# A decoder layer's output projection as seven half-size products

## The chip, the cores and the metric

The kernel runs on one NeuronCore of a Trainium2 chip. The metric is the device time of one execution in microseconds, the median of several. TensorE is PE below (PEld is its weight load), VectorE DVE, ScalarE ACT, GpSimd POOL, and SyncE, which issues most DMAs, SP.

## The reference, cut

One layer of a decoder for 1024 positions of 1024 channels in float32. Two gated feed-forward parts stand around a mixer of three branches, whose gated sum goes through one output projection.

```python
x = x + 0.5 * swiglu(rmsnorm(x, ffn1_norm), ffn1_w_gu, ffn1_w_down)
h = rmsnorm(x, mix_norm)
z = h @ w_in
...
merged = (gates[:, :, 0] * (y_a @ w_branch_a)
          + gates[:, :, 1] * (y_b @ w_branch_b)
          + gates[:, :, 2] * (y_c @ w_branch_c))
x = x + merged @ w_out
x = x + 0.5 * swiglu(rmsnorm(x, ffn2_norm), ffn2_w_gu, ffn2_w_down)
```

## The kernel before

**Layout.** Channels lie on the 128 partitions and positions along the free dimension: a matrix of 1024 x 1024 is eight row tiles `d` (or `c`) of 128 channels, each in two halves `half` (or `f`) of 512 positions. A float32 product is made of three matmuls of rounded parts (`mm3`, line 145): each operand is split into a high part (a cast on ACT, line 134) and a low part (a subtraction on DVE, line 135), and hi x hi, hi x lo and lo x hi are summed in one PSUM bank. One `mm3` is three matmuls of 128x128 by 128x512.

**Stages.** `run` (line 1008) goes through the first feed-forward part, the input projection with its gates (`Gates.run`, line 1513), the mixer (line 916: branch A, branch C, the attention of branch B, then branch B's product), the output projection (`project`, line 978), and the second feed-forward part. The feed-forward parts and the gates already use seven products of half-size blocks in place of eight (`Seven`, line 1171): with blocks of weights a11, a12, a21, a22 and of operands b11, b21, ..., sums s1 to s4 of weights and t1 to t4 of operands are made first, and seven products are added into the four blocks of the result.

**Branch B and the projection.** At the end of the mixer, for each row tile d and half f, four `mm3` (`branch`, line 551) make one bank. DVE multiplies it with the gate (`bsig`, line 973), POOL adds the sum of the other two branches (`bm`, line 974), and the result is split into `merged[f][d]`, which lies in the 16 `h` buffers. `project` then makes, for each half and each of eight columns c, a sum over eight `mm3` in one bank, adds it to the residual row (line 989), feeds the square into the norm's sum (`norm.feed`: a square on ACT, an addition on DVE, line 358) and stores the row. `w_out` is loaded and split twice, once for each half. After half 0, four tasks are put between the columns of half 1: the token sums (line 361), the turning of the scale (line 373), and the norm and split of half 0's rows.

**The second feed-forward part** begins with `units` (line 1283): for three units (two columns of weights each) the products s3·t3 and s4·b22, which need half 0 alone, are made first, while half 1's sums, scale and operands are made.

**What sets the order.** In a `manual_schedule` block the engines named keep the program's order. Elsewhere, in the mixer and in `project` among others, the compiler's planner orders each engine's instructions by its own estimate of when each is ready, program order breaking ties. Buffers come from pools: a tile asks for any free buffer of its tag, and waits if none is free. The pools here: `h` 16 and `x` (`x4`) 10 buffers of 128x1024; `raw` 3, `whi` and `wlo` 5 each of the same size; `t` (`row`) 6 of 128x512; `w4` 11 of 128x1024, in the feed-forward parts alone; PSUM has 4 single banks `one` and 4 `bank`. The attention's output keeps 8 of the 10 `x` buffers until branch B's product has ended. All the loads in this part go through SP's queue in order.

Of the kernel before, what the change touches and what calls it, by code (L numbers as in the profile page):

```python
# [9 lines left out]
F32 = mybir.dt.float32  # L10
F32R = mybir.dt.float32r
# [6 lines left out]
P = 128  # L18
# [31 lines left out]
class Kernel:  # L50
# [35 lines left out]
    def wide(self, tag):  # L86
        return self.wp.tile([P, D], F32R, name=tag, tag=tag, bufs=5)
# [828 lines left out]
    def mixer(self, norm):  # L916
# [45 lines left out]
        merged = [self.hrows() for _ in range(2)]  # L962
        with tc.tile_pool(name="bp", bufs=4) as p:
            w = {}
            for d, f in [(d, f) for d in range(DT - 3) for f in range(2)] + [(d, f) for f in range(2) for d in range(DT - 3, DT)]:
                if d not in w:
                    w[d] = self.load(a["w_branch"][1, d])
                sig, m = (p.tile([P, 512], F32, name=n) for n in ("bsig", "bm"))
                nc.sync.dma_start(sig, self.sig[DT + d][:, f])
                nc.sync.dma_start(m, mc[d, f])  # L970
                b = self.bank()
                self.branch(b, w[d], yb, f)
                nc.vector.tensor_tensor(sig, sig, b, op=ALU.mult)
                nc.gpsimd.tensor_tensor(sig, sig, m, op=ALU.add)
                self.split(*merged[f][d], sig)
        return merged

    def project(self, merged, norm, sink):

        nc, a = self.nc, self.a  # L980
        tasks = []
        for half in range(2):
            for c in range(DT):
                w = self.load(a["w_out"][c])
                b = self.bank()
                for k in range(DT):
                    self.mm3(b, w[k], merged[half][k], k == 0, k == DT - 1)
                x = norm.x(half, c)
                nc.vector.tensor_tensor(x, x, b, op=ALU.add)
                norm.feed(half, c)  # L990
                sink(half, c)
                if tasks:
                    tasks.pop(0)()
            tasks = norm.first() if half == 0 else tasks
        for t in tasks:
            t()
# [11 lines left out]
    def run(self):  # L1008
# [38 lines left out]
        with self.banks("mixps") as self.pm:  # L1047
            merged = self.mixer(norm)
        with tc.tile_pool(name="f2", bufs=1) as fp, self.banks("f2ps") as self.pm:
            rows = Rows(self)  # L1050
            for half in range(2):
                for p in range(DT // 2):
                    nc.sync.dma_start(rows.take(half, p), x1d[half, p])
            norm = OpNorm(self, rows, lambda: self.g_ffn2)
            ffn = SwiGLU(self, a["ffn2_w_gu"], a["ffn2_w_down"], fp, norm, 2)
            for f in range(2):
                ffn.fetch(f, [ffn.w4] * 4)
            ffn.fetch(2, [ffn.w4, self.x4] * 2)
            self.project(merged, norm, lambda half, c: keep(x2d, norm.t, half, c))
            E = mybir.EngineType  # L1060
            with tc.manual_schedule(engines={E.PE, E.DVE, E.Activation}):
                t1 = [ffn.w4] * 3 + [self.x4]
                ffn.units(
                    (0, 1), extra=2, kinds=(self.single, self.single, self.bank, self.bank, self.bank),
                    late=1, turn=2, rooms=lambda dt: t1.pop(0)(dt))
# [22 lines left out]
class OpNorm:  # L1088
# [11 lines left out]
    def feed(self, half, c):  # L1100
        self.acc[half] = self.k.norm_feed(self.acc.get(half), self.x(half, c), 512)
# [69 lines left out]
class Seven:  # L1171
# [54 lines left out]
    def product(self, out, w, name, op, first=True):  # L1226
        for j in range(4):
            m = tuple(x[:, j % 2] for x in self.norm.op[op][j // 2])
            s = tuple(x[:, j * P:(j + 1) * P] for x in w[name])
            self.k.mm3(out, s, m, first and j == 0, j == 3, skip_group_check=True)  # L1230

# [729 lines left out]
```

## Time and profile before

| | us |
|---|---|
| median of 3 runs | 2208.12 |
| lowest, highest | 2205.59, 2212.95 |
| the profiled execution, its own time | 2207.62 |
| the span of its trace | 2205.5 |

The trace is of one execution, the one of 2207.62 us; about 2.1 us of it lie outside the span. The page gives the busy time of each engine. A matmul's duration (0.39 us) overlaps that of the next, so that PE's pace is read from the starts. In a row of the timeline stand the start, the duration, the engine, the line, the operation, out<-in by name, the sizes, the count merged, and in brackets the idle time before it with what ended it. In a row of a group stand the count, then the busy time and the mean of one in ns, then the idle time before. In the list of DMAs the last figures are the size of one and the median time from issue to landing.

Branch B's product is at 1437.8 to some 1481 us of the trace, the projection from there to 1570.1, and the second feed-forward part follows.

### The profile page before, as it was taken

What the parts mean: (1) busy time and instruction counts of PE and PEld (TensorE: products, weight loads), DVE (VectorE), ACT (ScalarE), POOL (GpSimd) and SP (SyncE); (2) the same over time, 40 slices, a digit from 0 to 9 for tenths busy, and PEclk for the clock granted to TensorE, in tenths of its full rate; (3) what the DMA queues carried; (4) which work ended last, traced back from release to release, by engine and by line L of the source; (5) the groups of instructions that cost most, each with busy time, mean ns of one, the idle gap of its engine ahead of it and who ended that gap; (6) DMA issues with size and microseconds to landing.
All of it is one profiled execution on the core that took longest, in us unless ns stands there. A gap on an engine that the chain in (4) does not pass through costs nothing.

```text
span 2205.5 us, 27222 instructions
## 1 busy us (share of the span) xinstructions
PE 2176.3 (99%) x10192; PEld 1806.9 (82%) x10192; DVE 1536.0 (70%) x2252; ACT 901.5 (41%) x1385; POOL 243.3 (11%) x250
## 2 busy tenths in 40 slices
PE   8999999999999999999999999999999999999999
PEld 4778888888888888888878879988888888888887
DVE  7966566569889547555687779876886665656964
ACT  5432222233445335432366459833432222224332
POOL 0121212110000000000001431140021121211000
PEclk9999999999999999999999999999999999999999
DMA  4243333394432353324345660076033233338442
GB/s 154 69 133 95 115 101 113 108 330 147 149 123 94 117 172 116 133 96 148 114 149 194 190 222 31 28 259 251 29 115 115 91 110 101 115 122 322 138 139 95
DMA packets 124627, 300.05 MB, mean 136 GB/s; under 512 B 14096, under 2 KB 22288, under 8 KB 124496
## 3 DMA queue, kind: packets, MB, share of 16 engines
q1 hardware_dynamic: 121808, 295.17, 40.2%
q10 hardware_dynamic: 2688, 3.15, 0.4%
q8 instruction: 80, 1.31, 0.3%
q14 instruction: 51, 0.42, 0.1%
HBM read 209.01 MB, written 89.26 MB: 135 GB/s over the span
## 4 chain that ended last, share of the span: by engine, by line
PE 87%; DVE 9%; DMA 2%; issue 1%; ACT 1%; POOL 0%; SPq 0%; POOLq 0%; DVEq 0%; ACTq 0%
PE one L148 14%; PE one L150 14%; PE one L149 14%; PE bank L150 11%; PE bank L148 11%; PE bank L149 11%; DVE wlo L135 2%; PE mm L148 2%; PE mm L150 2%; PE mm L149 2%; PE bank L856 1%; PE bank L871 1%; PE bank L872 1%; DVE h L135 1%; PE bank L406 1%
## 5 line engine op out<-in xcount | busy, mean ns | idle before, releaser
L134 ACT CAST whi<-x 128x1024 fp32r<-128x1024 f32 (+1 forms) x213 | 200.6, 947 | 527.6 <-PE one L149 223.7
L1233 DVE TENSOR_TENSOR t<-t,one 128x512 f32<-128x512 f32 x149 | 102.3, 687 | 256.3 <-PE one L150 256.2
L148 PE MATMUL bank<-h,whi 128*128 128x512 f32 x688 | 268.9, 392 | 2.1 <-ACT t L1259 1.7
L150 PE MATMUL bank<-h,wlo 128*128 128x512 f32 x688 | 268.6, 391 | 0.0
L149 PE MATMUL bank<-h,whi 128*128 128x512 f32 x688 | 268.6, 390 | 0.0
L135 DVE TENSOR_TENSOR wlo<-x,whi 128x1024 fp32r<-128x1024 f32 (+1 forms) x213 | 234.0, 1102 | 39.5 <-ACT whi L134 39.3
L135 DVE TENSOR_TENSOR wlo<-w,whi 128x1024 fp32r<-128x1024 f32 (+1 forms) x153 | 168.4, 1115 | 75.5 <-ACT whi L134 75.4
L134 ACT CAST whi<-w 128x1024 fp32r<-128x1024 f32 (+1 forms) x153 | 142.6, 955 | 175.3 <-PE one L149 107.9
L148 PE MATMUL one<-h,whi 128*128 128x512 f32 x496 | 194.2, 392 | 1.8 <-ACT t L1259 1.2
L150 PE MATMUL one<-h,wlo 128*128 128x512 f32 x496 | 193.2, 389 | 0.5 <-DVE wlo L135 0.5
L149 PE MATMUL one<-h,whi 128*128 128x512 f32 x496 | 193.0, 389 | 0.0
L150 PE MATMUL one<-w,wlo 128*128 128x512 f32 x432 | 168.4, 390 | 0.4 <-DVE wlo L135 0.4
L148 PE MATMUL one<-w,whi 128*128 128x512 f32 x432 | 168.5, 390 | 0.0
L1233 DVE TENSOR_TENSOR raw<-t,one 128x512 f32<-128x512 f32 x130 | 89.2, 687 | 105.1 <-PE one L150 99.7
L148 PEld LDWEIGHTS bank<-h,whi 128*128 128x128 f32 x688 | 129.6, 188 | 29.2 <-ACT t L1259 2.2
L150 PEld LDWEIGHTS bank<-h,wlo 128*128 128x128 f32 x688 | 129.5, 188 | 27.0
L149 PEld LDWEIGHTS bank<-h,whi 128*128 128x128 f32 x688 | 129.5, 188 | 26.5
L1710 POOL TENSOR_TENSOR raw<-raw 128x512 f32<-128x512 f32 x39 | 81.1, 2078 | 591.4 <-DVE raw L1569 346.4
L148 PE MATMUL one<-whi 128*128 128x512 f32 x368 | 143.4, 390 | 0.0
L149 PE MATMUL one<-wlo,whi 128*128 128x512 f32 x368 | 143.2, 389 | 0.0
L150 PE MATMUL one<-whi,wlo 128*128 128x512 f32 x368 | 143.2, 389 | 0.0
L149 PE MATMUL one<-w,whi 128*128 128x512 f32 x356 | 138.5, 389 | 0.0
(364 smaller groups left out, 4701.2 us busy)
## 6 DMA issues: line engine op xcount, KB each, us to landing
x<-in_ffn_w_gu_dram SPq DMA_DIRECT2D x76, 512.0 KB, 4.4
w<-tdt SPq DMA_DIRECT2D x40, 512.0 KB, 3.7
gate<-raw SPq DMA_DIRECT2D x36, 512.0 KB, 3.0
tdb<-raw SPq DMA_DIRECT2D x64, 256.0 KB, 2.0
w<-tdb SPq DMA_DIRECT2D x30, 512.0 KB, 6.8
h<-in_ffn_w_down_dram SPq DMA_DIRECT2D x28, 512.0 KB, 6.3
x<-in_w_in_dram SPq DMA_DIRECT2D x26, 512.0 KB, 6.2
tdt<-w SPq DMA_DIRECT2D x44, 256.0 KB, 2.0
```

The lines of the kernel that those rows point to most:

```text
L134: self.nc.scalar.copy(hi, src)
L135: return (eng or self.nc.vector).tensor_tensor(lo, src, hi.bitcast(F32), op=ALU.subtract)
L148: mmul(out, s[0], m[0], start=first, stop=False, **kw)
L149: mmul(out, s[0], m[1], start=False, stop=False, **kw)
L150: self.last = mmul(out, s[1], m[0], start=False, stop=last, **kw)
L406: nc.tensor.transpose(b[:m, k * P:(k + 1) * P], s, self.ident)
L856: nc.tensor.transpose(b[:, at:at + P], prs[t][:, kk * P:(kk + 1) * P], self.ident)
L871: nc.tensor.matmul(o, w, pt[0], start=n == 0, stop=False)
L872: nc.tensor.matmul(o, w, pt[1], start=False, stop=n == len(pts) - 1)
L1233: return self.nc.vector.tensor_tensor(out, x, y, op=ALU.add)
L1710: sub = lambda d, x, y: nc.gpsimd.tensor_tensor(d, x, y, op=ALU.subtract)
```

## The change

The output projection becomes seven products of half-size blocks over all row tiles. The two dimensions that are halved are the 1024 channels summed over (row tiles j and j + 4) and, in the result, the columns c and c + 4; the operand's two halves of positions f are its two block columns. Each product is four outputs u of four `mm3`, 16 `mm3`.

- **Weight sums.** `out_sums` is called after gate units 4, 5, 6 and 7. It loads two column tiles of `w_out`, makes s1 to s4 on POOL, stores s2 and s3 in DRAM as they are, splits s1 and s4 on ACT and DVE, and stores their parts.
- **Branch B** moves into the scope of the second feed-forward part. `branch_b` goes over four pairs of row tiles j and j + 4. It loads the branch's weights for both tiles at once, in a `whi` buffer. After the pair's half 0 the operands b11 and b21 are split into `w4` buffers; after half 1, POOL makes two differences, DVE one, and t2, t3, t4, t1 and b22 are split.
- **`project`** makes a11·b11, a12·b21, s2·t2, s3·t3, a22·t4 (the last in `close`), then s1·t1 and s4·b22 by column. The first, third, fourth and fifth share four `one` banks, which hold running sums that are added to the rows after each product. The weights are asked for some pairs ahead. The second feed-forward part's loads, weight sums and splits are put between the products.
- **`close`** lies in the hand-ordered block: the fifth product, and the last two with half 0's token sums, scale, norm and operands between them. The square sums of most rows are added on POOL in place of DVE.
- **`units`** opens in another order, s4·b22 of two units first, and half 1's token sums stand in the middle of the second product.

```diff
+    def branch_b(self, yb, mc, w4):
...
+        op = {n: [None] * 4 for n in ("b11", "b21", "t1", "t2", "t3", "t4", "b22")}
+        rooms = iter([self.x4, self.x4, self.raw, self.raw, self.raw, self.x4, self.x4, self.raw])
+        rooms2 = iter([w4, w4, w4, self.x4])
...
+        def put(room, src, *names):
+            hi, lo = room(F32R), room(F32R)
+            self.split(hi, lo, src)
+            for i, n in enumerate(names):
+                op[n][j] = hi[:, i], lo[:, i]
+
+        for j in range(4):
+            raw = self.wide("whi", F32)
...
+            hi, lo = self.wide("whi"), self.wide("wlo")
+            self.split(hi, lo, raw)
+            s = []
+            for f in range(2):
+                s.append(two(next(rooms)()))
+                for i in range(2):
+                    d = j + 4 * i
+                    x, m = s[f][:, i], self.row()
+                    nc.sync.dma_start(x, self.sig[DT + d][:, f])
+                    nc.sync.dma_start(m, mc[d, f])
+                    b = self.bank()
...
+                    nc.vector.tensor_tensor(x, x, b, op=ALU.mult)
+                    nc.gpsimd.tensor_tensor(x, x, m, op=ALU.add)
+                if f == 0:
+                    put(w4, s[0], "b11", "b21")
+            if j % 2 == 0:
+                t2 = [next(rooms2)(F32R) for _ in range(2)]
+            t = self.row()
+            nc.gpsimd.tensor_tensor(s[1][:, 0], s[1][:, 0], s[0][:, 0], op=ALU.subtract)
+            nc.gpsimd.tensor_tensor(t, s[1][:, 1], s[1][:, 0], op=ALU.subtract)
+            nc.vector.tensor_tensor(s[0], s[0], t.unsqueeze(1).to_broadcast([P, 2, 512]), op=ALU.subtract)
+            op["t2"][j] = tuple(x[:, j % 2] for x in t2)
+            self.split(*op["t2"][j], t)
+            put(self.h4, s[0], "t3", "t4")
+            put(self.h4, s[1], "t1", "b22")
...
+        def product(out, n, u, t, first=False, mid=None):
+            while todo and (u % 2 == 0 and todo[0] in ahead[n, u // 2] or (n, u) not in ws):
+                weights(*todo.pop(0))
+            w = ws.pop((n, u))
+            for j in range(4):
+                self.mm3(
+                    out, tuple(x[:, j * P:(j + 1) * P] for x in w), op[t][j],
+                    first and j == 0, j == 3, skip_group_check=True)
...
+        def add(half, c, b, last=False, eng=nc.gpsimd):
+            x = norm.x(half, c)
+            nc.vector.tensor_tensor(x, x, b, op=ALU.add)
+            if last:
+                norm.feed(half, c, eng)
                 sink(half, c)
...
+        p = [self.single() for _ in range(4)]
+        for u in range(4):
+            product(p[u], "a11", u, "b11", True)
+            add(0, u, p[u])
+        for u in range(4):
+            b = self.bank()
+            product(b, "a12", u, "b21", True)
+            add(0, u, b, True)
+        ffn.fetch(0, [ffn.w4] * 4)
+        ffn.fetch(1, [ffn.w4] * 4)
+        for u in range(4):
+            product(p[u], "s2", u, "t2")
+            add(1, u, p[u])
...
+        for u in range(4):
+            product(p[u], "s3", u, "t3")
+            add(1, u + 4, p[u])
+            if u in (1, 3):
+                ready(u // 2)
...
+        def close():
+            for u in range(4):
+                product(p[u], "a22", u, "t4")
+                add(0, u + 4, p[u], True, v if u == 3 else nc.gpsimd)
+                if u == 0:
+                    ffn.sums(2)
...
+            one(0)
+            add(1, 4, end[0], True)
+            one(1, mid=lambda: norm.sums(0))
+            add(1, 5, end[1], True)
+            two(0)
+            norm.turn(0)
+            add(1, 0, end[0], True)
+            high()
+            one(2)
+            add(1, 6, end[2], True)
+            two(1)
+            low(0)
+            lo = cast(0)
+            add(1, 1, end[1], True)
+            one(3)
+            add(1, 7, end[3], True)
+            lo()
+            low(1)
+            two(2)
+            lo = cast(1)
+            add(1, 2, end[2], True, v)
+            two(3)
+            add(1, 3, end[3], True, v)
+            lo()
...
+    def out_sums(self, u, rooms):
...
+        a1, a2, sa, sb = (t() for t in rooms)
...
+        g = nc.gpsimd.tensor_tensor
+        g(s3, a21, a11, op=ALU.subtract)
+        g(s2, a22, s3, op=ALU.add)
+        g(s4, a12, s2, op=ALU.subtract)
+        g(s1, a21, a22, op=ALU.add)
+        for i, n in enumerate(("s2", "s3")):
+            nc.sync.dma_start(k.wo[n, 0, u // 2][:, u % 2], sa[:, i])
+        parts = [k.wide(y).rearrange("p (a w) -> p a w", a=2) for y in ("whi", "wlo")]
+        k.split(*parts, sb)
+        for i, n in enumerate(("s1", "s4")):
+            for part, x in enumerate(parts):
+                nc.sync.dma_start(k.wo[n, part, u // 2][:, u % 2], x[:, i].bitcast(F32))
...
                 self.unit(f)
+                turn = [x4, w4, x4, w4], [x4] * 4
+                if MEM_AT > f >= MEM_AT - 4:
+                    self.out_sums(f - MEM_AT + 4, turn[(last - f + 1) % 2])
```

157 lines of the change are left out of this document (101 added, 56 removed).

## The prediction

> **What bounds the kernel now.** I read the page's busy shares first, then who made PE wait, then stretches of some 22 us across the part that changes.
>
> ```profile
> span 2205.5 us, 27222 instructions
> PE 2176.3 (99%) x10192; PEld 1806.9 (82%) x10192; DVE 1536.0 (70%) x2252; ACT 901.5 (41%) x1385; POOL 243.3 (11%) x250
> ```
>
> PE is busy for all but 29 us of the span. Over 1500 to 1640 us, the output projection and the start of the second feed-forward part, the view of waits has two lines for PE, 0.4 us together; over 1437 to 1500 us it has none:
>
> ```profile
> PE one L148 <- DVE raw L1233: 0.2, 1, 0.2
> PE one L150 <- DVE wlo L135: 0.2, 1, 0.2
> ```
>
> By stretches (from:to, length, then busy time and count of PE, PEld, DVE, ACT, POOL, clock, DMA share, GB/s):
>
> ```profile
> 1437.00:1459.00 22.00, 22.00 (x103) 18.35 (x102) 12.66 (x18) 6.72 (x13) 8.51 (x6) 1.00 0.87 290
> 1459.00:1481.00 22.00, 22.00 (x98) 17.79 (x97) 18.04 (x23) 6.96 (x12) 11.48 (x9) 1.00 0.85 284
> 1481.00:1503.00 22.00, 22.00 (x99) 18.22 (x98) 15.31 (x21) 10.33 (x19) 5.43 (x4) 1.00 0.88 328
> 1547.00:1569.00 22.00, 22.00 (x99) 18.22 (x98) 20.32 (x28) 9.98 (x12) 0.00 (x0) 1.00 0.12 48
> ```
>
> PE is full in every one, so fewer matmuls shorten the span, and any new wait of PE lengthens it. What the reader is to see beside that: DVE is nearly full in two rows (18.0 and 20.3 of 22 us), and DMA in the first three. There the change adds work.
>
> **The change part by part.** PE's pace is read from starts in its timeline, since durations overlap:
>
> ```profile
> 1436.96 0.60 PE L891 MATMUL bank<-ident,t 128*128 128x128 f32 x4
> 1437.32 0.36 PE L872 MATMUL bank<-wlo,h 128*128 128x256 f32 x1
> 1437.76 0.40 PE L148 MATMUL bank<-x,whi 128*128 128x512 f32 x1
> ...
> 1570.08 0.39 PE L148 MATMUL one<-h,whi 128*128 128x512 f32 x1
> ...
> 1575.29 0.39 PE L150 MATMUL one<-h,wlo 128*128 128x512 f32 x1
> 1575.52 0.94 PE L367 MATMUL bank<-ones,t 128*128 128x1 f32 x8
> ```
>
> The rows at 1570.08 and 1575.29 are first and last of two products of 12: 5.21 us over 23 steps, 0.2265 us each.
>
> *Removed.* The old projection issues 2 halves x 8 columns x 8 x 3 = 384 matmuls of 128x512, the new one 7 products x 4 x 4 x 3 = 336. 48 x 0.2265 = **10.9 us** off PE. Branch B keeps its 192, and the token sums and scale transposes keep their number. With PE's waits here at 0.4 us, the rest of the change can win no more than that; each further term is a loss, or nothing.
>
> *Weight sums between the gates (`out_sums`, four times).* Each adds four POOL operations, one 1024-wide split on ACT and DVE, and 8 DMAs on SP's queue.
>
> ```profile
> 740.00:760.00 20.00, 20.00 (x90) 16.57 (x89) 10.39 (x13) 7.98 (x11) 0.00 (x0) 1.00 0.42 152
> ...
> 758.97 1.05 ACT L134 CAST whi<-x 128x1024 fp32r<-128x1024 f32 x1 [1.04 <-PE one L149]
> ...
> 778.01 1.05 ACT L134 CAST whi<-x 128x1024 fp32r<-128x1024 f32 x1 [1.04 <-PE one L149]
> ```
>
> In this stage POOL is idle, DVE half busy, and DMA at 0.42. A unit of 84 matmuls takes 19.0 us, and the cast at 758.97 is the first weight of the unit that begins about 778: a lead of one unit, set by the five `whi` buffers. The sums borrow one of the five, so each split slips by one release of PE, three products of 2.72 us at most; a lead of some 10 us stays. Behind the ACT cast that waits for POOL stand the next unit's casts, behind the stores on SP its loads: that lead covers both. If it is gone, a unit waits for a split or two, 1 to 3 us. I take **0.3** (0 to 3).
>
> *Start of branch B.* The weights now land in a `whi` buffer, which attention uses too, in place of `raw`, and two column tiles come at a time.
>
> ```profile
> 1433.87 0.38 PE L871 MATMUL bank<-whi,h 128*128 128x256 f32 x1 [0.61 <-DVE wlo L135]
> ...
> 1433.88 0.65 ACT L134 CAST whi<-raw 128x512 fp32r<-128x512 f32 x1
> ```
>
> ```profile
> bsig<-gate SPq DMA_DIRECT2D x16, 256.0 KB, 4.6
> raw<-in_w_out_dram SPq DMA_DIRECT2D x16, 512.0 KB, 4.9
> ```
>
> The first cast came 3.9 us before PE needed it. If a buffer comes free only about 1433.9, the load (4.9), the cast and the low part make it about 1441, 3.2 us late; if one of the five is free before, nothing is. The other loads (gates, branch sums) need no room of attention any more. I take **0.2** (0 to 3.2), nearer to nothing, since a buffer was at hand for the cast at 1433.88.
>
> *Operand sums behind branch B.* Per pair of column tiles j, PE has 48 matmuls, 10.9 us. The durations:
>
> ```profile
> L974 POOL TENSOR_TENSOR bsig<-bsig,bm 128x512 f32<-128x512 f32 x16 | 24.1, 1519 | 25.2 <-DVE bsig L973 15.5 <-DMA bm<-mc 7.9 <-ACT whi L134 1.9
> L973 DVE TENSOR_TENSOR bsig<-bsig,bank 128x512 f32<-128x512 f32 x16 | 10.9, 680 | 7.6 <-DMA bsig<-gate 7.6
> L134 ACT CAST h<-x 128x1024 fp32r<-128x1024 f32 x8 | 8.3, 1049 | 17.4 <-DVE x L1119 14.2 <-DVE x L1147 3.2
> ...
> 1590.98 2.35 DVE L1155 TENSOR_TENSOR x<-x,x 128x1024 f32<-128x1024 f32 x2
> ```
>
> DVE does, from PSUM, four multiplications (4 x 0.68 = 2.7); between SBUF tensors, five of 1024 (weight low part, three operand low parts, S minus t; 1.17 each, half the pair at 1590.98) and one of 512: 6.5. POOL does six of 512, four sums and two differences. ACT's 4.8 hide. The next rows show that POOL and DVE don't run side by side on SBUF:
>
> ```profile
> 1449.32 2.60 POOL L974 TENSOR_TENSOR bsig<-bsig,bm 128x512 f32<-128x512 f32 x2 [7.88 <-DMA bm<-mc]
> 1453.14 1.67 POOL L974 TENSOR_TENSOR bsig<-bsig,bm 128x512 f32<-128x512 f32 x1 [1.22 <-DVE bsig L973]
> ...
> 1451.30 1.17 DVE L135 TENSOR_TENSOR h<-bsig,h 128x512 fp32r<-128x512 f32 x1 [0.76 <-ACT h L134]
> ...
> 1452.98 2.38 DVE L135 TENSOR_TENSOR wlo<-raw,whi 128x512 fp32r<-128x512 f32 x2
> ...
> 1493.08 1.28 DVE L135 TENSOR_TENSOR wlo<-raw,whi 128x512 fp32r<-128x512 f32 x2
> ```
>
> Two low parts take 1.28 us while POOL idles (1493.08) and 2.38 with a POOL sum between them (1452.98): 1.28 plus most of POOL's 1.30 (half of the row at 1449.32). So per j the two engines need up to 6.5 + 6 x 1.30 = 14.3 us one after the other, against PE's 10.9. The Trainium skill states this as a rule, against this change: "SBUF — State Buffer", section "Who interferes with whom", says that a DVE instruction with two SBUF inputs and a GpSimd instruction that reads SBUF exclude each other for a whole instruction. By that rule the trace agrees; it makes of branch B 57 us of shared work instead of two loads that fit.
>
> Call T the end of branch B on PE: 1437.76 + 192 x 0.2265 = 1481.2. The deadline is `b11` of j = 3: the first product reads it at its tenth matmul, T + 2.0. If PE's order, which the compiler's planner lays down here, puts the first three j of all four outputs ahead, it is T + 8.2; that the planner mixes is seen where L891 stands between parts of L871/L872. The last tile pair goes into the third `x4` room asked for while branch B's operands hold eight of ten, so its load waits until j = 2's sums are split. Side by side: PE ends j = 2 at T - 10.9, plus 0.7 + 1.3 + 1.3 + 1.05 + 1.17, so the room is free at T - 5.4; load 4.6; multiply, two sums, cast, low part 5.5; ready at T + 4.7. With POOL and DVE excluding each other, from the first sum at 1441.2 on: three j are done at 1441.2 + 42.9 - 1.2 = T + 1.7, and `b11` is ready at T + 11.8. The stall lies between nothing (early, mixed order) and 9.8 us (late, program order). I take **1.8**: the late end misses the mixed deadline by 3.6, and half of that is the middle. Everything later (`t2` at T + 21.8, `t3` at T + 32.6) has room; so have the row loads, which start when branch B's operands go, at T, and are first needed on PE's path when the s2 product writes over the first outputs, T + 21.8.
>
> *The closing stretch.* It is ordered by hand on PE, DVE and ACT. From half 0's scale transposes to half 1's token sums, now in the middle of the second opening product, PE has about 17.7 us (6 products and 18 matmuls, less the bit that the transposes take).
>
> ```profile
> 1537.77 5.35 DVE L1119 SCALAR_TENSOR_TENSOR x<-x,c_ffn_norm,bank 128x512 f32<-128x512 f32 x8
> ...
> 1570.28 0.69 DVE L989 TENSOR_TENSOR x<-x,bank 128x512 f32<-128x512 f32 x1 [1.75 <-PE bank L150]
> 1572.01 0.69 DVE L358 TENSOR_TENSOR t<-t 128x512 f32<-128x512 f32 x1 [1.05 <-ACT t L353]
> ...
> 1576.50 0.16 DVE L174 TENSOR_SCALAR rms_v<-bank 128x4 f32<-128x4 f32 x1 [3.80 <-PE bank L367]
> ```
>
> DVE has there: 8 norm rows (5.4), five of 1024 ahead of the last square sum (5.9), six additions (4.1), two square sums (1.4): 16.8, and two waits of 1.05 for ACT's squares, 18.9 in all. So it just misses, and the square sums that move to POOL come on top: 6 x 1.3 = 7.8 us in which low parts are shut out. In the old kernel DVE stood idle 3.8 us before the row at 1576.50; that idle time is the only cover. Bounds 0 (sums of POOL fall into DVE's PSUM work) and 7.8; I take **1.5**, nearer to the low end since 9.5 us of DVE's work reads PSUM.
>
> *The sum.* -10.9 + 0.3 + 0.2 + 1.8 + 1.5 = -7.1. The profiled execution took 2207.62 us, span 2205.5 with 2.1 around it: 2207.6 - 7.1 = **2200.5**. It lies 0.5 under the median shown, 2208.12, within the runs' spread.
>
> **The rivals.**
> *Nothing stalls.* The planner mixes and POOL falls into gaps: 2207.6 - 10.9 = 2196.7. For it: four banks and a full PE throughout before. Against it: the 14.3 us per j.
> *The excluded engines, in program order.* This is the rule cited above at work: `b11` comes at T + 10 to T + 11.8 and PE waits some 8 us: 2207.6 - 10.9 + 8 + 2 = 2206.7, no change. For it: the doubled low parts at 1452.98. Against: a planner free to mix.
> *DVE late in the closing stretch.* 5 us in place of 1.5: 2204. For it: 20.3 of 22 us busy in that place already.
> *Slower.* The chain of branch B, strictly one after the other: if in addition the PSUM multiplications (2.7 per j) find no gap beside POOL, three j take 3 x 17.0, the room for j = 3 is free at T + 9.8, its operands at T + 19.9, and PE in program order waits 17.9: 2207.6 - 10.9 + 17.9 + 2 = 2216.6. It decides from a stall of 15.5 us on. Against it: L973 keeps its 680 ns beside POOL, so those do overlap.
>
> **How the numbers follow.** A measurement of this kernel tells about 0.3%, 6.6 us, from no change. Chances: forecast 0.42 (its own range 2198.5 to 2203), nothing stalls 0.22, program order 0.15, late closing 0.10, slower 0.11. Faster means under 2201.5: all of the second and 0.27 of the forecast's, 0.49; within 0.40; slower 0.11. The range goes from the clean case, less 0.7 for the runs' spread, 2196, to 2209, program order at its full 9.8 us; the slow case is left out.
>
> **What would show it.** Right: 336 projection matmuls at 0.2265 us, PE's waits between branch B and the second feed-forward part of about 4 us, one at the first product for a low part in `w4` (where `b11` lies), one at the token sums; L135 well over 1.2 us wherever POOL is busy; nothing between the gates. Wrong: no PE wait at the first product (the planner hid it), PE waiting for `whi` among the gates, or a wait for a DMA of x2d, x1d or weights in the crowded first 45 us, which I cost at nothing because before it, at 0.85 to 0.88 DMA share, no PE wait named one.

## The result and the profile after

| | us |
|---|---|
| before, median of 4 runs | 2208.86 (2205.59 to 2212.95) |
| after, median of 4 runs | 2219.74 (2217.44 to 2224.18) |
| ratio after to before | 1.0051, 95% interval 1.0027 to 1.0074 |
| spans of the two profiled executions | 2205.5 and 2215.7 |

The kernel became slower by 10.9 us; the prediction was 2200.5, and its range ended at 2209. The head of the page after:

```profile
span 2215.7 us, 27178 instructions
PE 2173.8 (98%) x10144; PEld 1801.3 (81%) x10144; DVE 1553.1 (70%) x2235; ACT 903.4 (41%) x1363; POOL 300.7 (14%) x285
```

PE has 48 instructions less, as it should, and is busy for less time, yet the span is 10.2 us longer: the matmuls that went were paid for by idle time. The stretches of the prediction again (length, busy time and count of PE, PEld, DVE, ACT, POOL, clock, DMA share, GB/s), with the one behind them:

```profile
1437.00:1459.00 22.00, 21.66 (x121) 18.76 (x120) 15.17 (x20) 10.22 (x16) 8.99 (x8) 1.00 0.70 239
1459.00:1481.00 22.00, 21.52 (x95) 17.48 (x94) 17.43 (x16) 6.30 (x7) 15.89 (x10) 1.00 0.22 72
1481.00:1503.00 22.00, 17.29 (x67) 13.02 (x66) 15.88 (x15) 6.71 (x7) 13.93 (x9) 0.92 0.71 249
1503.00:1525.00 22.00, 18.34 (x74) 14.47 (x73) 15.52 (x17) 10.16 (x13) 6.95 (x6) 0.92 0.91 322
1547.00:1569.00 22.00, 22.00 (x104) 18.31 (x104) 14.84 (x30) 6.54 (x9) 6.84 (x5) 1.00 0.71 240
```

Where PE was full there are now 4.7 and 3.7 us of idle time in the third and fourth rows, and the granted clock falls to 0.92. From 1459 to 1481 the DMA share is 0.22: the loads that are missed at 1490 could have been made there. The view of waits from 1437 to 1640 us (what PE waited for, us, times, the longest):

```profile
PE one L148 <- ACT whi L134: 3.5, 2, 2.0
PE one L150 <- DVE wlo L135: 2.3, 1, 2.3
PE bank L367 <- DVE t L358: 2.0, 1, 2.0
PE bank L148 <- ACT whi L134: 1.7, 1, 1.7
PE bank L148 <- DVE x L996: 0.9, 1, 0.9
PE bank L148 <- DVE raw L996: 0.5, 1, 0.5
```

`whi` and `wlo` are parts of weights, so 7.5 us are waits for weights and none for the operands that I had feared; 1.4 us are waits for banks that DVE had not emptied, 2.0 us for the token sums.

The offset of like instructions against the kernel before adds up the whole: 0.3 us on entering the gates, 3.1 behind them, 4.7 after the memory attention (1133 us), 5.6 at branch B's first matmul:

```profile
1443.38 0.39 PE L148 MATMUL bank<-x,whi 128*128 128x512 f32 x1
```

That row stood at 1437.76 before. From there to 1630 us the offset goes to 10.2: -10.9 for the matmuls, 10.9 of waits, some 1.6 in which PE starts up again after seven of them (at each the overlap of 0.39 - 0.23 = 0.16 us is lost, and the next start comes 0.1 late where the clock is full), and some 3.0 of a thing that was not in my sum. PE's timeline shows it:

```profile
1495.31 0.40 PE L148 MATMUL one<-w,whi 128*128 128x512 f32 x1
1498.04 0.50 PE L150 MATMUL one<-w,wlo 128*128 128x512 f32 x1 [2.33 <-DVE wlo L135]
...
1499.29 0.63 PE L148 MATMUL one<-w,whi 128*128 128x512 f32 x1
1499.72 0.63 PE L149 MATMUL one<-w,whi 128*128 128x512 f32 x1
...
1502.25 0.39 PE L150 MATMUL one<-w,wlo 128*128 128x512 f32 x1
1502.48 0.39 PE L148 MATMUL one<-w,whi 128*128 128x512 f32 x1
```

Behind the wait the starts are 0.43 us apart in place of 0.23, for 3.4 us, and then at full pace again: half clock, which costs some 1.6 us (eight steps of 0.43 in place of 0.23). A second such stretch follows at 1515.8, of which 0.5 us falls into a wait. The same is in the mixer's memory attention, 1130 to 1134 us, in after and not in e1 (below), whose code there is that of before (1.6 us). After, then e1:

```profile
1130.00:1134.00 4.00, 4.00 (x19) 3.82 (x19) 2.74 (x4) 4.00 (x12) 0.00 (x0) 0.57 0.23 66
```

```profile
1130.00:1134.00 4.00, 3.14 (x21) 2.82 (x22) 3.91 (x8) 4.00 (x13) 0.00 (x0) 1.00 0.11 29
```

### The profile page after: what moved, and what is told of

Same layout as the page of the kernel before. It is cut to its first block, busy times and chain, and to the rows that moved or that the text cites. A ratio compares the mean times of both kernels' runs of the same rounds, so it can differ in the third digit from the quotient of the medians.

```text
span 2215.7 us, 27178 instructions
## 1 busy us (share of the span) xinstructions
PE 2173.8 (98%) x10144; PEld 1801.3 (81%) x10144; DVE 1553.1 (70%) x2235; ACT 903.4 (41%) x1363; POOL 300.7 (14%) x285
## 4 chain that ended last, share of the span: by engine, by line
PE 56%; DVE 3%; DMA 2%; ACT 1%; POOL 1%; issue 1%; SPq 0%; POOLq 0%; ACTq 0%; DVEq 0%
PE one L148 9%; PE one L150 9%; PE one L149 9%; PE bank L150 6%; PE bank L148 6%; PE bank L149 6%; PE mm L148 2%; PE mm L150 2%; PE mm L149 2%; PE bank L856 1%; PE bank L871 1%; PE bank L872 1%; PE bank L406 1%; DVE wlo L135 1%; DMA raw<-in_w_out_dram 0%
## 5 line engine op out<-in xcount | busy, mean ns | idle before, releaser
L1382 DVE TENSOR_TENSOR t<-t,one 128x512 f32<-128x512 f32 x149 | 102.2, 687 | 253.9 <-PE one L150 253.8
L135 DVE TENSOR_TENSOR wlo<-x,whi 128x1024 fp32r<-128x1024 f32 (+1 forms) x215 | 239.5, 1118 | 43.2 <-ACT whi L134 37.9
L148 PE MATMUL bank<-h,whi 128*128 128x512 f32 x592 | 232.0, 393 | 2.1 <-ACT t L1408 1.7
L149 PE MATMUL bank<-h,whi 128*128 128x512 f32 x592 | 231.4, 391 | 0.0
L150 PE MATMUL bank<-h,wlo 128*128 128x512 f32 x592 | 231.1, 391 | 0.0
L148 PE MATMUL one<-h,whi 128*128 128x512 f32 x528 | 206.9, 392 | 4.0 <-DVE t L1382 2.5
L150 PE MATMUL one<-h,wlo 128*128 128x512 f32 x528 | 205.7, 389 | 0.5 <-DVE wlo L135 0.5
L149 PE MATMUL one<-h,whi 128*128 128x512 f32 x528 | 205.6, 389 | 0.0
L148 PE MATMUL one<-w,whi 128*128 128x512 f32 x464 | 181.7, 393 | 3.5 <-ACT whi L134 3.5
L150 PE MATMUL one<-w,wlo 128*128 128x512 f32 x464 | 181.6, 392 | 2.7 <-DVE wlo L135 2.7
L1382 DVE TENSOR_TENSOR raw<-t,one 128x512 f32<-128x512 f32 x130 | 89.2, 687 | 96.7 <-PE one L150 91.9
L149 PE MATMUL one<-w,whi 128*128 128x512 f32 x380 | 149.1, 392 | 0.0
L148 PEld LDWEIGHTS bank<-h,whi 128*128 128x128 f32 x592 | 111.6, 188 | 25.4 <-ACT t L1408 2.2
L150 PEld LDWEIGHTS bank<-h,wlo 128*128 128x128 f32 x592 | 111.7, 189 | 23.3
L149 PEld LDWEIGHTS bank<-h,whi 128*128 128x128 f32 x592 | 111.7, 189 | 22.8
```

The source lines that it names most:

```text
L135: return (eng or self.nc.vector).tensor_tensor(lo, src, hi.bitcast(F32), op=ALU.subtract)
L148: mmul(out, s[0], m[0], start=first, stop=False, **kw)
L149: mmul(out, s[0], m[1], start=False, stop=False, **kw)
L150: self.last = mmul(out, s[1], m[0], start=False, stop=last, **kw)
L1382: return self.nc.vector.tensor_tensor(out, x, y, op=ALU.add)
```

## The experiments

Theory W: the time is lost where the change takes buffers that others need, `whi` and `wlo` among the gates, `raw` in branch B. Rivals: X, POOL and DVE shutting each other out of SBUF; Y, a crowded DMA; Z, the clock and the planner's order. Each kernel was timed 5 to 11 times beside the kernel before, whose median was 2207.81 to 2208.66 there; ratios are to that.

| kernel | median us | ratio to before, 95% interval |
|---|---|---|
| after_again | 2218.91 | 1.0045 (1.0031 to 1.0059) |
| e1_sums_alone | 2210.72 | 1.0011 (1.0001 to 1.0020) |
| e2_no_sums | 2213.28 | 1.0023 (1.0014 to 1.0032) |
| e3_parts_in_place | 2215.69 | 1.0025 (1.0013 to 1.0038) |
| e4_raw_free | 2213.16 | 1.0019 (1.0008 to 1.0029) |
| e5_both | 2210.05 | 1.0008 (0.9999 to 1.0017) |
| e6_third_room | 2210.63 | 1.0010 (1.0001 to 1.0019) |
| e7_differences_dve | 2210.56 | 1.0004 (0.9994 to 1.0014) |
| e8_no_differences | 2204.36 | 0.9977 (0.9969 to 0.9986) |
| e9_nofill | 2207.22 | 0.9992 (0.9984 to 1.0001) |
| e9_fill | 2210.11 | 1.0012 (1.0003 to 1.0020) |
| e10_late_parts | 2210.20 | 1.0010 (1.0001 to 1.0019) |
| e11_late_parts_dve | 2207.73 | 0.9996 (0.9987 to 1.0005) |
| e12_forced_order | 2209.50 | 1.0005 (0.9996 to 1.0014) |
| e13_forced_dve | 2204.37 | 0.9980 (0.9971 to 0.9989) |
| e14_sums_later | 2202.93 | 0.9974 (0.9963 to 0.9985) |

### The changed kernel once more

> The changed kernel once more, so that it has as many runs as the experiments that are set against it. Theory (its 2219.7 is what it costs): 2217 to 2222. Rival (half clock comes by the phase in which a run starts, and its first four runs were unlucky): 2213 to 2216; the gains of e3 and e4 against it would then be 4 to 5 us smaller than they look.

2218.91: the loss is no matter of four unlucky runs.

### The weight sums: alone, left out, and without their two buffers

> The kernel before plus the four calls of out_sums among the gates; the stored sums are read by nobody, the output projection is the old one. Theory W (what was lost ahead of branch B, 5.8 us, is the price of the sums: their split holds one buffer of `whi` and one of `wlo` until its stores have landed, and DVE waits in order): slower than before by 2.8 us in the gates, with PE waiting about twice for the additions of L1382's kind between 770 and 815 us, and by up to 5.8 us at branch B's start if the mixer's shift hangs on it too. Rival Z (clock and planner, not the sums): no more than 0.7 us, and no PE wait between 700 and 860 us beyond the 0.7 us of before.

```diff
+                if MEM_AT > f >= MEM_AT - 4:
+                    self.out_sums(f - MEM_AT + 4, turn[(last - f + 1) % 2])
```

> The changed kernel without out_sums: the weight blocks of s1 to s4 are loaded from w_out's own blocks and from the memory keys' parts instead of the sums, same sizes, same rooms, so the output is not the reference's. Theory W: 2.8 us (up to 5.8) faster than the changed kernel, so 2214 to 2217, and the PE waits for weights between 1485 and 1520 stay as they were (about 10 us with the half clock behind them). Rival Z: within 0.7 us of the changed kernel, the gates without waits but something else as late at branch B.

```diff
-                    nc.sync.dma_start(x, self.wo[n, part, q])
+                    nc.sync.dma_start(x, self.mkv["mk"][part].rearrange("p (c w) -> p c w", c=2))
...
-                nc.sync.dma_start(two[0], self.wo[n, 0, q])
+                nc.sync.dma_start(two[0], a["w_out"][2 * q:2 * q + 2, :, 4:].rearrange("c p k w -> p c (k w)"))
...
-                if MEM_AT > f >= MEM_AT - 4:
-                    self.out_sums(f - MEM_AT + 4, turn[(last - f + 1) % 2])
```

> The changed kernel, with the parts of s1 and s4 written into the sums' own rooms (a1, a2) instead of a `whi` and a `wlo` buffer; nothing else differs. Theory W: the two PE waits of 1.4 us in the gates go, 2.8 us faster than the changed kernel, about 2217, and DVE has no wait for a store into wo_s any more. Rival (POOL's sums shut DVE out of SBUF, whoever holds the buffers): the two waits stay, since the collisions of POOL L1622 with DVE L135 stay; within 0.7 us of the changed kernel.

```diff
-        parts = [k.wide(y).rearrange("p (a w) -> p a w", a=2) for y in ("whi", "wlo")]
+        parts = [y.bitcast(F32R) for y in (a1, a2)]
         k.split(*parts, sb)
```

In after the chain is seen in DVE's timeline, and in DVE's waits from 700 to 860 us:

```profile
768.21 1.22 DVE L135 TENSOR_TENSOR wlo<-x,whi 128x1024 fp32r<-128x1024 f32 x1 [1.28 <-DMA wo_s<-wlo]
...
771.15 2.32 DVE L135 TENSOR_TENSOR wlo<-x,whi 128x1024 fp32r<-128x1024 f32 x1 [0.39 <-ACT whi L134]
773.39 0.67 DVE L1382 TENSOR_TENSOR t<-t,one 128x512 f32<-128x512 f32 x1
```

```profile
DVE wlo L135 <- DMA wo_s<-wlo: 5.2, 4, 3.1
```

The low part of a gate unit's weights waits for a `wlo` buffer that is still being stored to DRAM. DVE takes its work in order, so the addition of L1382, which empties PE's bank, comes late behind it, and PE waits. e1 has the same chain with the old projection: there DVE waits 6.3 us in three places for such stores, and PE 2.8 us in two for the additions. PE's waits in that stretch, in after and then in e3:

```profile
PE one L148 <- DVE t L1382: 2.2, 2, 1.1
PE bank L149 <- DVE wlo L135: 0.8, 1, 0.8
```

```profile
PE bank L149 <- DVE wlo L135: 0.7, 1, 0.7
```

In e3 the sums, their stores and POOL's collisions with DVE are all there (POOL's first sum stretches a low part to 2.28 us at 771.71), but the two waits are gone, and with them 3.2 us of the changed kernel's median when it was run again, 4.1 of the first; W had said 2.8. (The two intervals overlap a little; the waits that went are what shows it.) One thing was expected otherwise: DVE still waits 3.3 us in two places for the sums' stores in e3, now ahead of a later sum (L1359), at no cost to PE. e1 puts the price of the sums alone at 2.1 us against before, under W's 2.8 to 5.8, though its interval holds 2.8. e2 takes 5.6 us off the changed kernel by leaving them out. Taking fewer buffers, as e3 does, pays for nearly all of the gates: the offset behind them, against before, is 3.1 us in after, 0.6 in e3 and 0.1 in e5, which has the same edit. What e2 has beyond e3, 2.4 us, does not come from the gates, where neither loses time, and was not followed up.

### Room for the weights

> The changed kernel, with two of branch B's four pairs in `raw` (j=2 f=0 and j=3 f=1, the ones held past branch B's end) moved to `wlo` buffers; j=1's two stay in `raw`. Theory W (weight loads had no room): PE's waits for whi and wlo at the first two products, 7.5 us, and the 2.7 us of half clock behind them go; 8 to 10 us faster than the changed kernel, 2210 to 2212. Rival X (POOL and DVE shut each other out, the operands are late as well): PE waits as long for b11 of j=3 instead, and less than 3 us is won. Rival Y (the DMA queues are full, loads take 6 to 11 us whenever they start): the first wait shrinks by some 2 us, the ones at 1511 to 1516 stay; 2 to 4 us won.

```diff
-        rooms = iter([self.x4, self.x4, self.raw, self.raw, self.raw, self.x4, self.x4, self.raw])
+        low = lambda: self.wide("wlo", F32)
+        rooms = iter([self.x4, self.x4, self.raw, self.raw, low, self.x4, self.x4, low])
```

SP's queue in after (start, time to issue, line, what), then in e4:

```profile
1469.01 2.27 SPq L993 DMA_DIRECT2D t<-mc  x4
1480.55 0.79 SPq L992 DMA_DIRECT2D raw<-gate  x2
1482.76 0.38 SPq L1030 DMA_DIRECT2D raw<-in_w_out_dram  x1
...
1489.32 5.18 SPq L1030 DMA_DIRECT2D raw<-in_w_out_dram  x2
```

```profile
1473.18 0.38 SPq L1031 DMA_DIRECT2D raw<-in_w_out_dram  x1
...
1481.38 2.12 SPq L1031 DMA_DIRECT2D raw<-in_w_out_dram  x2
```

In after the queue stands from 1471.3 to 1480.55 at the load of the pair j = 3, f = 1, which waits for a `raw` buffer, and the loads of `w_out` stand behind it. In e4 they go out 8 to 9.6 us earlier (branch B begins 1.1 earlier), and the waits from 1437 to 1640 us become:

```profile
PE one L148 <- ACT w L134: 4.0, 1, 4.0
PE bank L367 <- DVE t L358: 2.0, 1, 2.0
PE bank L148 <- DVE x L997: 1.7, 2, 1.0
PE bank L148 <- DVE wlo L997: 0.4, 1, 0.4
```

All 7.5 us of waits for weights are gone: W is right, and Y falls, since the row loads are as many as before. But a wait of 4.0 us for `w` stands in their place: the operand b11 of j = 3, the very wait that the prediction bounded. In after it was hidden, since PE had stood for the weights already. (e13, below, waits only 1.7 us there, and has no wait for weights either.) The gain is 5.8 us against the second timing of the changed kernel, short of W's 8 to 10, with X's part left.

> e3 and e4 in one kernel: the parts of s1 and s4 in the sums' own rooms, and j=2 f=0 and j=3 f=1 in `wlo` instead of `raw`. Theory W: the two causes lie in different stages and add up: 4.05 + 6.6 us off the changed kernel's 2219.7, so 2209 (2207 to 2211), no change against before; left over are PE's wait for the operands of j=3 in `w4` (4.0 us in e4), the waits for banks in branch B (2.1), the one for the token sums (2.0) and half clock. Rival (both gains were the same pauses of the clock, and don't add up): 2212 to 2214.

The two edits together give 2210.05: they add up, and the kernel is level with before.

### The operands: rooms, engine, order or amount

> e5 with the pair of j=3 f=0 in a `whi` buffer instead of the third `x4` room. Theory W2 (that room is late: in e4 the gate loads of this pair went out at 1489.9, behind SP's wait for it, and its multiplications came at 1496.4 and 1498.7, some 8 us after PE was done): PE's wait of 4.0 us for `w` goes or falls under 1 us, with 1.7 us of half clock behind it; 4 to 6 us under e5, so 2203 to 2205. Rival X (POOL and DVE shutting each other out is what makes the operands late, the room adds nothing): PE still waits 3 us or more for `w`, and the gain is under 1.5 us.

```diff
+        high = lambda: self.wide("whi", F32)
-        rooms = iter([self.x4, self.x4, self.raw, self.raw, low, self.x4, self.x4, low])
+        rooms = iter([self.x4, self.x4, self.raw, self.raw, low, self.x4, high, low])
```

A miss: the third `x4` room, on which the prediction's late bound rested in part, was not the cause. The gate's tile comes in time, PE begins the first product sooner, and then waits the same 4.0 us for `w`, from 1485.7 on.

> e6 with the two differences of each j (s1 minus s0, and t) on DVE instead of POOL. Theory X (each POOL operation of 1.3 us shuts DVE out, where the same on DVE takes 0.68): the excluded work of a j falls from 14.3 to some 12.9 us, the DVE waits for banks at the end of branch B (2.1 us in after and e4) fall to 1 us or less, 1 to 2 us under e6. Theory W2 alone (rooms decide, the engines have slack): within 0.7 us of e6; if DVE is the bound, slower, by up to 2 us, with longer waits for banks.

```diff
-            nc.gpsimd.tensor_tensor(s[1][:, 0], s[1][:, 0], s[0][:, 0], op=ALU.subtract)
-            nc.gpsimd.tensor_tensor(t, s[1][:, 1], s[1][:, 0], op=ALU.subtract)
+            nc.vector.tensor_tensor(s[1][:, 0], s[1][:, 0], s[0][:, 0], op=ALU.subtract)
+            nc.vector.tensor_tensor(t, s[1][:, 1], s[1][:, 0], op=ALU.subtract)
```

> e6 without the three difference operations of each j (two on POOL, one on DVE of 1024); the products get the sums that are there instead, so the output is not the reference's. It prices the new operand sums: theory X: the waits for banks in branch B go altogether, with any rest of the wait for `w`: 2 to 4 us under e6. Theory W2: within 1 us of e6, since the low parts and room loads set the pace.

```diff
-            t = self.row()
-            nc.gpsimd.tensor_tensor(s[1][:, 0], s[1][:, 0], s[0][:, 0], op=ALU.subtract)
-            nc.gpsimd.tensor_tensor(t, s[1][:, 1], s[1][:, 0], op=ALU.subtract)
-            nc.vector.tensor_tensor(s[0], s[0], t.unsqueeze(1).to_broadcast([P, 2, 512]), op=ALU.subtract)
+            t = s[1][:, 1]
```

e7 cannot be told from e6. Its two waits for the operand `w` are 2.6 and 2.1 us. e8, which has no differences at all, is 6.3 us faster than e6; its wait for `w` is 1.4 us, and no bank of branch B is waited for. That is more than the 2 to 4 us that X gave it, and the first thing that brings the kernel under the one before.

> e6 with the operand parts that are needed last (t3, t4, t1, b22 of a j, two splits of 1024 into `h`) put behind the b11 and b21 parts of the next j. Theory X1 (the shared time of POOL and DVE is spent in the wrong order: in e6 two of these low parts, 4.2 us, stood ahead of the split that PE waited for): PE's wait of 4.0 us for `w` falls to 1 us or less and half clock behind it with it; 3 to 6 us under e6, 2205 to 2207.5. Rival X2 (the sum of the excluded work is what counts, whatever its order): the wait goes to a later operand (t2, t3) or to branch B's banks, less than 1.5 us is won.

```diff
-            put(self.h4, s[0], "t3", "t4")
-            put(self.h4, s[1], "t1", "b22")
+            later.append(lambda s=s, j=j: put(self.h4, s[0], "t3", "t4", j=j))
+            later.append(lambda s=s, j=j: put(self.h4, s[1], "t1", "b22", j=j))
```

e10 decides nothing: the planner gave DVE the order of e6 again around the wait. The rows of e6 that e10 was to change:

```profile
1483.21 1.23 DVE L1007 TENSOR_TENSOR wlo<-wlo,t 128x1024 f32<-128x1024 f32 x1 [1.96 <-POOL t L1006]
...
1484.95 0.68 DVE L998 TENSOR_TENSOR whi<-whi,bank 128x512 f32<-128x512 f32 x1
1485.56 1.93 DVE L135 TENSOR_TENSOR h<-wlo,h 128x1024 fp32r<-128x1024 f32 x1
1487.41 2.28 DVE L135 TENSOR_TENSOR h<-x,h 128x1024 fp32r<-128x1024 f32 x1
```

DVE stands 1.96 us for POOL's difference while the multiplication of j = 3 (L998) is queued behind it, and then two low parts that nobody needs yet collide with the sums that PE is waiting for.

> e10 with the two differences of each j on DVE, as in e7. X1: as e10 within 1 us, since order and not the engine decides. X2: 1.5 us or more under e10, since the excluded work of a j is 1.4 us less.

e11 is e10 with the edit of e7. It gives 2207.73, with waits for `w` of 2.9 and 0.5 us: 2.5 us under e10, as X2 has it, but the two intervals overlap. Then the order was fixed by marks, first alone, then with less for POOL:

> e6 with DVE's order of the operand sums fixed by explicit order marks: for j = 0 to 2 the subtraction s0 minus t comes only behind the two f = 0 multiplications of the next j, and the low parts for `h` only behind the low part of the next j's b11 and b21. The differences stay on POOL. Theory X1 (DVE waited in order for POOL's t, 2 us each time, with the multiplications of the next j behind it; the order is what costs): PE's wait of 4.0 us for `w` falls to 1.5 us or less, with the half clock behind it, the bank waits go; 3 to 5 us under e6's 2210.6, so 2205.5 to 2207.5. Theory X2 (the amount of excluded work decides): less than 1.5 us under e6, the wait moves on to t2, t3 or the weights.

```diff
+            def rest(j=j, s=s, t2=t2, t=t):
+                i = nc.vector.tensor_tensor(s[0], s[0], t.unsqueeze(1).to_broadcast([P, 2, 512]), op=ALU.subtract)
+                if j < 3:
+                    self.after(i, last["mult"])
...
+                    i = put(self.h4, src, *names, j=j)
+                    if j < 3:
+                        self.after(i, last["low"])
+            later.append(rest)
```

> e12 with the two differences of each j on DVE, behind the next j's multiplications too, so that POOL has only four sums of 512 for each j and DVE never waits for POOL's t. X1: within 1 us of e12. X2: 1.5 to 3 us under e12, since the excluded work of a j falls from 14.3 to 12.9 us and the chain has two POOL operations less; 2204 to 2206.

```diff
-            diffs = [
-                nc.gpsimd.tensor_tensor(s[1][:, 0], s[1][:, 0], s[0][:, 0], op=ALU.subtract),
-                nc.gpsimd.tensor_tensor(t, s[1][:, 1], s[1][:, 0], op=ALU.subtract)]
...
+                i = nc.vector.tensor_tensor(s[1][:, 0], s[1][:, 0], s[0][:, 0], op=ALU.subtract)
+                if j < 3:
+                    self.after(i, last["mult"])
+                nc.vector.tensor_tensor(t, s[1][:, 1], s[1][:, 0], op=ALU.subtract)
```

e12 gives 2209.5, 1.1 us under e6 and within the intervals; its wait for `w` is 3.5 us. The marks did what they were to do: from 1443 to 1495 us DVE's waits for POOL's `t` fall from 5.9 us in e6 to 0.9. But e12 does not test order alone, since one more thing is late in it. POOL's sums at 1489.73 waited 2.24 us for `mc`, whose loads stood in SP's queue behind loads of `w_out` that waited for `raw` buffers, and went out at 1484.61, against 1481.07 in e6. SP's queue in e12, then POOL:

```profile
1470.90 13.61 SPq L1047 DMA_DIRECT2D raw<-in_w_out_dram  x3
1484.61 1.82 SPq L997 DMA_DIRECT2D t<-mc  x4
```

```profile
1489.73 2.48 POOL L1001 TENSOR_TENSOR whi<-whi,t 128x512 f32<-128x512 f32 x2 [2.24 <-DMA t<-mc]
```

e13 gives 2204.37. Its edit differs from e12 in the two differences alone, which are now DVE's and stand behind the next j's multiplications too. The waits from 1437 to 1640 us in e13:

```profile
PE bank L367 <- DVE t L358: 2.0, 1, 2.0
PE one L148 <- ACT w L134: 1.7, 1, 1.7
PE one L149 <- DVE w L135: 0.6, 1, 0.6
```

Of the two, X2 is the nearer: e13 is 5.1 us under e12, more than the 1.5 to 3 that X2 gave it. Order alone won too little to be told from nothing (e12), moving the differences alone as well (e7), both together 6.3 us. What of it won the time stays open. Against e12, e13 has less work on which the engines exclude each other, two hand-overs to POOL less in the chain, and no late `mc` ahead of the sums that PE waits for. e7 was late by `mc` too: DVE waited for no POOL sum there, but POOL's sums waited 11.1 us in three places for `mc`, 3.2 of them ahead of the pair behind which PE then stood 2.6 us. In e12 such waits are 4.5 us, in e13 2.5, in e8 none. Whether these loads decide is a rival that no run tests by itself. The collisions can be read in e13's timeline, DVE's rows and then POOL's:

```profile
1456.88 0.69 DVE L1011 TENSOR_TENSOR x<-x,x 128x512 f32<-128x512 f32 x1
1457.67 1.59 DVE L1014 TENSOR_TENSOR t<-x 128x512 f32<-128x512 f32 x1
```

```profile
1457.04 1.67 POOL L1001 TENSOR_TENSOR raw<-raw,t 128x512 f32<-128x512 f32 x1 [0.50 <-DVE raw L1000]
```

Of two subtractions of one size, the first, which began before POOL's sum, takes 0.69 us, and the second, beside the sum, 1.59 (the same line takes 0.68 at 1498.7, with POOL idle). The sum takes 1.67 in place of 1.29 at its shortest.

### Filling the wait

> e5 with the order of its first products written out: j = 0 to 2 of a11 for all four outputs, j = 0 to 2 of a12 for three, then the j = 3 parts. It is the control of e9_fill. All theories: as e5, 2210 (2208 to 2212), with a PE wait of about 4 us for the operands of j = 3 and half clock for 3.4 to 6.8 us behind it.

> e9_nofill with 14 matmuls of 128x512 into a bank that nobody reads, put between the j = 0 to 2 parts and the j = 3 parts, in the wait: 14 x 0.2265 = 3.2 us of work that isn't needed. Theory C (the half clock follows a pause of PE): the pause shrinks to under 1 us, the half clock between 1495 and 1515 us is gone, and the kernel is 1.7 to 3.4 us faster than e9_nofill although it computes more. Rival (the clock falls for another reason, such as the load on DMA or the other engines in this stretch): the half clock stays, and the time is that of e9_nofill within 1 us.

```diff
+        for i in range(14):
+            fill = self.nc.tensor.matmul(dummy, op["b11"][0][0][:, :P], op["b11"][0][0],
+                                           start=i == 0, stop=i == 13, skip_group_check=True)
+            if i == 0:
+                self.after(fill, self.last)
```

Both leave out the j = 3 part of three a12 products, 9 matmuls or 2.0 us of PE. The pair tells nothing of the clock: written out, the order broke the control's wait into pieces of 1.6 and 0.8 us, with no half clock behind them, so there was nothing to win. The fill moved a wait to the next banks (3.7 us for L1055 in place of 1.4) and cost 2.9 us, near the 3.2 of its matmuls.

### The token sums

> e13 with half 1's token sums behind the second opening product in place of its middle, six matmuls (1.36 us) later, and the scale transposes behind the fourth product in place of the third. Theory: PE's wait of 1.96 us for DVE's last square sum falls to 0.6 us, and half clock behind it comes less often: 1.4 to 3 us under e13, 2201.5 to 2203. Rival (the wait only moves, to the transposes or to the products that need half 1's operands): within 0.7 us of e13.

```diff
-                    late=1, turn=2, rooms=lambda dt: t1.pop(0)(dt),
+                    late=1, turn=3, rooms=lambda dt: t1.pop(0)(dt),
...
-            self.product(out, w[u], s, name, mid=middle if opening and n == late else None)
+            self.product(out, w[u], s, name, mid=None)
```

The waits from 1437 to 1640 us in e14, the three longest:

```profile
PE one L148 <- ACT w L134: 2.0, 1, 2.0
PE one L148 <- DVE raw L1398: 0.9, 1, 0.9
PE bank L367 <- DVE t L358: 0.6, 1, 0.6
```

The wait fell to 0.6 us as worked out, and 0.9 us came back at L1398. e14 is 1.4 us under e13, at the low edge of what was expected, and the two intervals overlap. It has the lowest median of all: 2202.93, 5.6 us under before, 0.9974 (0.9963 to 0.9985).

## Why the prediction was wrong

- **-10.9 for the matmuls**: right. The counts fell by 48, and where fewer waits are left (e14, 4.4 us) the kernel is faster.
- **Gates' weight sums, 0.3 (bounds 0 to 3)**: mis-sized; 2.8 in the offsets, 2.1 in e1, gone in e3. The step that failed is "each split slips by one release of PE ... a lead of some 10 us stays". A buffer that is stored to DRAM is free when the store has landed, not when PE has released it, and I had asked what stands behind ACT's cast and SP's stores, not what stands behind DVE's low part: the addition that frees PE's bank.
- **Start of branch B, 0.2**: right, nothing to be seen.
- **Operand sums, 1.8 (0 to 9.8)**: that the engines exclude each other was right (low parts of 1024 took 2.3 us beside POOL), and so was the mixed order (in after the four hi x hi of j = 3 start together at 1505.65). The waits came elsewhere: 1.4 us for banks, which I had not named, and none for b11, as it hid behind the weights. Uncovered, in e4 to e6, the wait for b11 is 4.0 us. That it is near my late bound for the mixed order (3.6) is in part luck, since that bound holds the 4.6 us load into the third `x4` room, and e6 shows that this room was not the cause.
- **Weights at nothing**: the step that failed most, 7.5 us. I named a wait for weights as what would make me wrong, and looked for its cause in the DMA share. It was room: the two pairs that stay in `raw` past the end of branch B (j = 2 f = 0 and j = 3 f = 1) leave one of three buffers for loads that are needed at T, and DMA was at 0.22 in the 22 us ahead of them. I counted `x` buffers and not `raw`, though the diff gives both lists.
- **Closing stretch, 1.5**: right, 2.0. The collision is there: two differences of 1024 (L1093) took 1.90 and 2.25 us beside POOL's square sums. In the working, the 17.7 us are five products and 18 matmuls, not six; the number is right.
- **Half clock and start-ups, not in the sum**: 3.0 us of half clock behind the waits of the projection, and 1.6 in the mixer; 1.6 of start-ups. A further 0.9 us was lost in the attention, where the planner's order differs from before; what of the change brought that was not tried (0.4 of it is in e1 too, with the old code there). So rival Z holds for 2.5 us of this profile.
- **The rivals**: the slower one came nearest, 2216.6, by luck, since its mechanism is not what happened; its chance of 0.11 was too low, since I had priced only the waits that I had thought of.

## What to carry to other kernels

Where a change uses shared buffers for something that lives longer, list for each tag who holds each buffer until when, stores included, and which loads stand behind that request in the queue. Where the bound engine is full, every wait that is added costs more than its length, by a start-up (0.2 us here) and at times a stretch of half clock. When two engines exclude each other, moving work to the one that does it in half the time may win nothing by itself; here it won only together with a new order, and the loads in the queue changed along with both.

## What the hardware showed that I had not expected

Half clock comes on a grid. In e3 there are five onsets between 1100 and 1640 us (from windows of 0.25 us; the clock is the third figure from the end):

```profile
1128.00:1128.25 0.25, 0.25 (x6) 0.25 (x4) 0.25 (x1) 0.25 (x1) 0.00 (x0) 0.96 0.00 0
1189.50:1189.75 0.25, 0.25 (x3) 0.21 (x2) 0.25 (x2) 0.25 (x2) 0.17 (x1) 0.84 0.96 381
1493.25:1493.50 0.25, 0.00 (x0) 0.00 (x0) 0.25 (x1) 0.00 (x0) 0.25 (x1) 0.92 0.84 311
1513.75:1514.00 0.25, 0.25 (x3) 0.20 (x2) 0.25 (x1) 0.25 (x2) 0.14 (x1) 0.88 0.99 377
1582.00:1582.25 0.25, 0.25 (x4) 0.25 (x3) 0.25 (x1) 0.25 (x1) 0.00 (x0) 0.91 0.78 311
```

A window at 0.96 was at half clock for 8% of its end, so the onsets are 1128.23, 1189.67, 1493.46, 1513.94 and 1582.20: 61.44, 303.79, 20.48 and 68.26 us apart, which is 18, 89, 6 and 20 times 3.413. Each lasts one or two such steps. The Trainium skill, "TensorE: Matmul & The Clock Gate", "Part 1: The HAM clock gate", tells of a free-running window of 3413 ns, and this case agrees to 0.01 us. It puts the slow state behind a window in which PE is idle; here less is enough, since the step ahead of 1498.8 in after held 2.33 us of waiting and over 1 us of matmuls.

So the price of one and the same wait depends on where it falls on the grid. The wait for the token sums was 1.9 to 2.0 us in 15 of the profiles with the changed projection: no half clock behind it in five, one step in seven, two steps in three, 0 to 3.2 us for a like pause, 1.4 on the mean (13 steps of 1.6 us in 15 profiles). Laid on each trace's own grid, the wait fell whole into one step in seven of the 15, and half clock followed in all seven. In the other eight a border cut it; half clock followed in three, where one step held 1.62 to 1.73 us of idle time, and not in five, with 1.08 to 1.71.

Counted over 1100 to 1640 us of all 18 profiles, 40 steps that began at full clock held over 1.85 us of idle time or of matmuls of one or 32 columns, and half clock followed every one. Such matmuls seem to count as idle: the step ahead of 1189.67 in e3 held no idle time, but 2.05 us of them. Of the 2766 steps with less, half clock followed 11, ten of them at one place of the mixer, with 1.57 us. The 1.6 us there are of this kind: the pause is the same 1.53 us for ACT in e1 and 1.54 in e2, and only e2's is followed by half clock.

Single profiles differ by several us along with this: e6's profiled execution took 2207.00 us, without half clock near 1128 and 1189 us, and its median is 2210.63. Over its eleven runs the mean clock goes from 0.998 in the shortest to 0.994 in the longest. So only medians over many runs can be set against each other. All this is counted from traces; that pauses cause half clock was not shown by an experiment, since e9 had nothing to tell.
